# Modulation chunks gathered in one PSUM bank per batch instead of one bank use per chunk

## The chip, the cores and the metric

The kernel runs on one core of a Trainium2 chip. A core has a matrix engine (PE), a vector engine (DVE), a scalar engine (ACT), a general engine (POOL), an engine that only issues transfers here (SP), and 16 DMA engines. Matmul results go to banks of PSUM, which DVE and ACT read; this kernel has one bank for `pf`, three for `ps` and two double ones for `pd`. Everything else lives in SBUF. The metric is the device time of one execution in microseconds.

## The reference, cut to what matters

The program is two blocks one after the other, over 256 tokens of width 1024: two "hybrid" layers, and then two conditioned layers, each with an attention (neighbourhood attention, then grouped-query attention) and a mixture of 32 experts. The change concerns the conditioning vector of the second block:

```
c_act = jax.nn.silu(c)
for i in range(DEPTH):
    mod = c_act @ ada_w[i] + ada_b[i]
    sh1, sc1, g1, sh2, sc2, g2 = jnp.split(mod[:, None, :], 6, axis=-1)
    h = x * (1 + sc1) + sh1
    ...
    x = layer_norm(DEEPNORM_ALPHA * x + (1 + g1) * y, ln_g[i, 0], ln_b[i, 0])
    h = x * (1 + sc2) + sh2
    ...
    x = layer_norm(DEEPNORM_ALPHA * x + (1 + g2) * y, ln_g[i, 1], ln_b[i, 1])
```

`c` is one row of 1024 numbers; `ada_w` is 2 x 1024 x 6144. So `mod` is two vector-matrix products: 48 MB of weights for 12,288 results, six sections of 1024 for each layer.

## The kernel before, in words

The stages follow each other: hybrid layer 0 (0 to 166 us), hybrid layer 1 (to 322), the neighbourhood layer (to 490), its experts (to 945), the grouped-query layer (to 1090), and its experts. The modulation doesn't depend on the tokens, so it is worked off beside the other stages. Its weights are cut into 24 chunks of 2 MB, of 512 results each: chunk n belongs to layer n // 12, section n // 2 % 6, half n % 2.

A generator (`ada_cols`) makes two steps of a chunk: its load (L696), and its computation. Calls of `ada()` are spread over the layers, and a table (`ADA_PLAN`) says how many steps each call advances: the first four chunks lie in hybrid layer 0, 4 to 8 in layer 1 and at its end, 9 to 15 in the neighbourhood layer, 16 to 23 in the grouped-query layer. Within what these calls allow, a scheduler chooses the order on each engine when the program is built, and moves independent matmuls into gaps; only an instruction marked with `keep_in_program_order` stays where it is written. Loads go to buffers from a ring, so a load waits until the ones who used its buffer are done.

22 chunks are computed on PE (L706 to L727). The activated vector stands as the stationary operand `cact`, 128 x 32, each column the same. The 128 x 128 array is used as four column groups of 32: each group takes its 256 columns of the chunk and half of the depth (four matmuls of 128 rows), so 16 matmuls of 128x32 by 128x256 make a chunk. The profile counts two records for each, as the type is 32-bit. The result is 32 equal rows in each of the four groups, in the one bank `pf` that these uses share (L48: one buffer). DVE or ACT copies it to `parts` (L715). What remains is the tail (L718): two small matmuls with `sel`, a matrix of zeros and ones that adds the two depth halves and turns the row into columns, again through `pf`, and one DVE operation that adds the bias (and 1 for the scale sections) into `modc` (L723). A tail is held back until the next chunk has been copied (L716).

Two chunks (2 and 10, `ADA_ROWS`) are computed on DVE instead: four operations of 128x1024 that multiply the chunk by `crow` and sum (L701), and one that adds the bias (L702). `crow` is `c`, broadcast to all partitions by a transfer (L252) and activated by four ACT and eight DVE operations (L256 to L258).

`modc` is read by the feed of each layer, by `spread` (which makes rows out of a column vector with diagonal matrices, L747) and by `fold`, whose results POOL and DVE turn into the folded router weights in the same tile `parts` (L787, L788) and then into row sums by a matmul (L790). Split matmuls (`mm3`, L177) are those that multiply in three passes of high and low halves; transposes are L159, all other matmuls L162.

## Time and profile before

| | us |
|---|---|
| median of 3 runs | 1562.01 (1561.87 to 1565.70) |
| span of the profiled execution | 1560.8 |
| PE busy | 1231.1 (79%) |
| DVE busy | 569.4 (36%) |
| ACT busy | 356.6 (23%) |
| POOL busy | 236.6 (15%) |

The span goes from the first to the last instruction of the profiled execution; its own time is that span and about 1.2 us around it, if the median of the runs is taken for it. Busy times are sums over stages with different limits, so they don't say what bounds a stage. In the rows below, a group of matmuls is counted in records, and "[4.76 <-DVE parts L220]" means that the engine stood for 4.76 us before, and that a DVE instruction of line 220, writing the tile `parts`, released it.

### The profile page before, as it was taken

To read this page: it belongs to the slowest core of one execution; us is meant where nothing else is said; L and a number is where in the kernel's file an instruction comes from. 1 tells how busy PE (TensorE), PEld (TensorE's weight loads), DVE (VectorE), ACT (ScalarE), POOL (GpSimd) and SP (SyncE) were. 2 spreads that over 40 slices of the span, in tenths; PEclk is the share of its full clock that TensorE was granted. 3 is DMA by queue.
4 is the path that set the end of the run, shared out by engine and by line. 5 is a ranking of instruction groups with operands and counts; after the bars stand their busy time and mean duration, and the time that the engine had idled before them with its cause. 6 is when DMAs were issued, how large, how long until landed. Compare 5 with 4: busy or idle time off the path is not lost.

```text
span 1560.8 us, 24728 instructions
## 1 busy us (share of the span) xinstructions
PE 1231.1 (79%) x10584; PEld 789.8 (51%) x10584; DVE 569.4 (36%) x1258; ACT 356.6 (23%) x759; POOL 236.6 (15%) x283
## 2 busy tenths in 40 slices
PE   6898899999998986664877768889897764586774
PEld 6787788777967442321333326757543322243322
DVE  6677567555467210100111105877411100011113
ACT  5453443444442100000000004363100000010000
POOL 2721272122111200000000004320200000000000
PEclk9999999999999998876898889989999887798797
DMA  9436543468487999999999999575999999999995
GB/s 370 178 147 242 213 166 152 163 236 343 169 342 290 405 426 427 427 428 426 427 426 427 428 423 410 210 279 206 388 427 427 428 427 425 427 427 427 426 427 210
DMA packets 46705, 532.76 MB, mean 341 GB/s; under 512 B 7040, under 2 KB 10240, under 8 KB 15104
## 3 DMA queue, kind: packets, MB, share of 16 engines
q1 hardware_dynamic: 45440, 527.99, 82.2%
q10 hardware_dynamic: 1152, 3.15, 0.6%
q8 instruction: 85, 1.39, 0.4%
q14 instruction: 28, 0.23, 0.0%
HBM read 530.07 MB, written 1.05 MB: 340 GB/s over the span
## 4 chain that ended last, share of the span: by engine, by line
DMA 43%; PE 40%; DVE 9%; POOL 2%; ACT 2%; issue 2%; SPq 0%; DVEq 0%; ACTq 0%; POOLq 0%
DMA b<-in_moe_w_gate_up_dram 25%; DMA b<-in_moe_w_down_dram 16%; PE ps L162 14%; PE pd L177 9%; PE ps L177 8%; PE pf L162 3%; PE pd L162 3%; PE ps L159 3%; DMA b<-in_ada_w_dram 2%; DVE b L128 1%; ACT b L125 1%; POOL b L128 1%; POOL rs L196 0%; POOL rs L201 0%; DVE b L220 0%
## 5 line engine op out<-in xcount | busy, mean ns | idle before, releaser
L162 PE MATMUL ps<-b,b 128*32 128x256 f32 (+2 forms) x5248 | 484.6, 475 | 198.2 <-DMA b<-in_moe_w_gate_up_dram 138.9
L162 PEld LDWEIGHTS ps<-b,b 128*32 128x32 f32 (+1 forms) x5248 | 191.6, 120 | 432.1 <-issue 275.7
L177 PE MATMUL ps<-b,b 128*128 128x256 f32 (+1 forms) x1464 | 198.8, 295 | 6.6 <-DVE gates L565 5.6
L177 PEld LDWEIGHTS ps<-b,b 128*128 128x128 f32 x1464 | 186.7, 195 | 17.1 <-DVE gates L565 6.1
L177 PE MATMUL pd<-b,b 128*128 128x256 f32 (+2 forms) x1152 | 188.3, 320 | 4.6 <-ACT b L600 1.3
L177 PEld LDWEIGHTS pd<-b,b 128*128 128x128 f32 x1152 | 162.0, 196 | 25.3 <-issue 4.4
L128 POOL TENSOR_TENSOR b<-b,b 128x1024 fp32r<-128x1024 f32 (+2 forms) x46 | 115.5, 2517 | 348.2 <-ACT b L125 348.2
L125 ACT CAST b<-b 128x1024 fp32r<-128x1024 f32 (+1 forms) x124 | 126.1, 1035 | 160.2 <-PE ps L177 71.7
L226 ACT COPY b<-ps 128x256 f32<-128x256 f32 (+1 forms) x81 | 36.0, 449 | 456.4 <-PE ps L162 308.2
L128 DVE TENSOR_TENSOR b<-b,b 128x1024 fp32r<-128x1024 f32 x78 | 115.9, 1490 | 62.1 <-ACT b L125 57.0
L220 DVE COPY b<-ps 128x256 f32<-128x256 f32 (+1 forms) x71 | 36.2, 510 | 263.1 <-PE ps L162 214.1
L1115 POOL TENSOR_TENSOR b<-b,g 128x128 f32<-128x128 f32 x64 | 23.6, 399 | 595.1 <-PE ps L159 548.7
L1097 DVE SCALAR_TENSOR_TENSOR sl<-sl,ps 128x128 f32<-128x128 f32 x64 | 18.4, 288 | 248.4 <-ACT sl L1096 248.4
L159 PE MATMUL ps<-cst,b 128*128 128x128 f32 (+1 forms) x404 | 77.5, 302 | 39.7 <-DVE b L220 17.5
L159 PEld LDWEIGHTS ps<-cst,b 128*128 128x128 f32 (+1 forms) x404 | 45.3, 147 | 105.2 <-DVE b L220 34.7
L162 PE MATMUL pd<-b 64*128 64x512 f32 (+1 forms) x384 | 82.6, 552 | 15.4 <-DVE b L1145 12.9
L1145 DVE TENSOR_TENSOR b<-ps,parts 128x512 f32<-128x512 f32 x32 | 22.1, 692 | 180.8 <-PE ps L162 179.9
L162 PEld LDWEIGHTS ps<-b,x 128*128 128x128 f32 x512 | 68.3, 218 | 21.9 <-issue 18.4
L162 PE MATMUL ps<-b,x 128*128 128x128 f32 x512 | 72.2, 305 | 3.8 <-issue 1.6
L1096 ACT ACTIVATE sl<-ps 128x128 f32<-128x128 f32 x64 | 17.8, 278 | 236.9 <-PE ps L159 236.9
L162 PE MATMUL pf<-b,cact 128*32 128x256 f32 x704 | 56.0, 428 | 13.5 <-DVE modc L723 4.9
L162 PEld LDWEIGHTS pd<-b 64*128 64x128 f32 x384 | 34.3, 190 | 52.9 <-DVE b L1145 26.2
(304 smaller groups left out, 944.0 us busy)
## 6 DMA issues: line engine op xcount, KB each, us to landing
b<-in_moe_w_gate_up_dram SPq DMA_DIRECT2D x128, 2048.0 KB, 32.5
b<-in_moe_w_down_dram SPq DMA_DIRECT2D x62, 2048.0 KB, 35.3
b<-in_ada_w_dram SPq DMA_DIRECT2D x24, 2048.0 KB, 8.4
b<-in_w_in_dram SPq DMA_DIRECT2D x12, 2048.0 KB, 8.0
b<-in_na_w_qkv_dram SPq DMA_DIRECT2D x6, 2048.0 KB, 9.3
b<-in_gqa_w_qkv_dram SPq DMA_DIRECT2D x3, 2048.0 KB, 23.4
b<-in_w_out_dram SPq DMA_DIRECT2D x4, 1024.0 KB, 5.7
b<-in_w_out_dram SPq DMA_DIRECT2D x2, 2048.0 KB, 7.4
```

The lines of the kernel that those rows point to most:

```text
L125: S.copy(hi[:, s], v[:, s])
L128: (G if on_pool else e).tensor_tensor(lo[:, s], v[:, s], hi[:, s].bitcast(F32), OP.subtract)
L159: T.transpose(o, a, ident)
L162: return T.matmul(o, lhsT=a, rhs=b, start=start, stop=stop)
L177: T.matmul(o, lhsT=a[u], rhs=b[v], start=start and i == 0, stop=stop and i == 2)
L220: V.tensor_copy(o, i)
L226: S.copy(o, i)
L1096: S.activation(sl, ps[:, 0:128], AF.Tanh, scale=0.5)
L1097: V.scalar_tensor_tensor(sl, sl, 1.0, ps[:, 0:128], op0=OP.add, op1=OP.mult)
L1115: G.tensor_tensor(PG[:, t, :, du].rearrange("p q (e s) -> p q e s", e=2), P[:, t].rearrange("p (q e) s -> p q e s", q=2), g32[:, t, 4 * g: ...
L1145: V.tensor_tensor(do, ps, parts, OP.mult)
```

## The change

All 24 chunks are computed on PE, and chunks gather in batches: 0 to 6, 7 to 15, 16 to 23. The stationary operand is now a slice of a zero-padded tile `cz` (128 x 8 x 63) in which only column 31 holds the vector: the slice 31-s to 63-s has it in column s and zeros elsewhere. Chunk number s of a batch thus adds its result to row s of each column group and zeros to the others, and the bank `pf` is held from the first chunk of a batch to its last. Copy, tail matmuls and bias come once for each batch, in `flush`, with a wider `sel` (128 x 64); these two matmuls go to a `ps` bank. The 1 of the scale sections is added to the biases at the start. `crow`, its transfer and its activation go away. A call of `flush` is new at the end of the second hybrid layer; the other two stand where they stood.

```diff
-        if ADA_ROWS[n]:
-            w = w.rearrange("p (j k) -> p j k", j=4)
-            for j in range(4):
-                V.scalar_tensor_tensor(w[:, j], w[:, j], 1.0, crow, op0=OP.mult, op1=OP.mult, accum_out=o[:, j:j + 1])
-            V.scalar_tensor_tensor(o, o, one, b, op0=OP.add, op1=OP.add)
-            flush()
-            yield
-            return
         w = w.rearrange("p (k f) -> p k f", k=8)
-        part = parts[:, c * 256:c * 256 + 256]
-        first, ps = pin[0], PF()
+        s = len(batch)
+        if not s:
+            held[0] = PF()
+        batch.append(n)
         for k in range(4):
             for q in range(4):
                 kk, f0 = q % 2 * 4 + k, q // 2 * 256
-                i = mm(ps[32 * q:32 * q + 32, 0:256], cact[:, kk], w[:, kk, f0:f0 + 256], k == 0, k == 3)
+                i = mm(held[0][32 * q:32 * q + 32, 0:256], cz[:, kk, 31 - s:63 - s], w[:, kk, f0:f0 + 256],
+                       s == 0 and k == 0, n in ADA_LAST and k == 3)
-        evac(part, ps[:, 0:256])
-        flush()
...
-                mm(ps[:, 2 * i:2 * i + 2], a, sel, True, True)
-            V.scalar_tensor_tensor(o.rearrange("p (a i) -> p a i", i=2), ps[:, 0:4].rearrange("p (i a) -> p a i", i=2),
-                                   one, b.rearrange("p (a i) -> p a i", i=2), op0=OP.add, op1=OP.add)
```

The new `flush`:

```diff
+        n0, n = batch[0], len(batch)
+        acc, part, ps = held[0], parts[:, 0:256], PS()
+        evac(part, acc[:, 0:256])
+        for i in range(2):
+            mm(ps[:, i * 2 * n:(i + 1) * 2 * n].rearrange("p (a s) -> p a s", a=2), part[:, i * 128:i * 128 + 128],
+               sel[:, :, 0:n], True, True)
+        o = modc.rearrange("p l s k -> p (l s k)")[:, 4 * n0:4 * (n0 + n)]
+        b = col[:, K_ADA + 4 * n0:K_ADA + 4 * (n0 + n)]
+        V.tensor_tensor(o.rearrange("p (s a i) -> p s a i", a=2, i=2),
+                        ps[:, 0:4 * n].rearrange("p (i a s) -> p s a i", i=2, a=2),
+                        b.rearrange("p (s a i) -> p s a i", a=2, i=2), OP.add)
```

At the start:

```diff
-        nc.sync.dma_start(crow, p["c_2"].partition_broadcast(128))
-        for i in range(4):
-            c = crow[:, i * 256:i * 256 + 256]
-            S.activation(th, c, AF.Tanh, scale=0.5)
-            V.tensor_scalar(th, th, 0.5, 0.5, op0=OP.mult, op1=OP.add)
-            V.tensor_tensor(c, c, th, OP.mult)
...
-        V.tensor_copy(cact, csil[:, :, None].to_broadcast([128, 8, 32]))
+        V.memset(cz, 0.0)
+        V.tensor_copy(cz[:, :, 31], csil)
+        b = col[:, K_ADA:K_ADA + 96].rearrange("p (g n) -> p g n", g=4)[:, :, 8:24]
+        V.tensor_scalar(b, b, 1.0, None, op0=OP.add)
```

The order on PE changes in many places. The first shown is in the second hybrid layer, where PE waits for DVE's gates ahead of the next split matmuls (b_1585 and b_1573 are the layer's transposed input, b_2372 and b_2352 the weights of chunk 5, b_2567 and b_2541 those of chunk 6). Before:

```order
L177 MATMUL ps<-b_1585,b_83 128x256
L177 MATMUL ps<-b_1585,b_82 128x256 x2
L177 MATMUL ps<-b_1585,b_83 128x256
L177 MATMUL ps<-b_1585,b_82 128x256
L162 MATMUL pf<-b_2372,cact 32x256 x4
L177 MATMUL ps<-b_1585,b_82 128x256 [waits DVE_49]
```

Further on, before:

```order
L159 MATMUL ps<-cst,b_1553 128x128 [waits Activation_49]
L159 MATMUL ps<-cst,b_1553 128x128 x3
L159 MATMUL ps<-cst,b_1553 128x128 [waits DVE_49]
L159 MATMUL ps<-cst,b_1553 128x128 x3
L162 MATMUL pf<-b_2567,cact 32x256 [waits DMAHW7_49]
L162 MATMUL pf<-b_2567,cact 32x256 x15
L177 MATMUL ps<-b_1585,b_82 128x256 [waits DVE_49,Activation_49]
```

With the change:

```order
L177 MATMUL ps<-b_1573,b_82 128x256
L177 MATMUL ps<-b_1573,b_81 128x256
L162 MATMUL pf<-b_2352,cz 32x256 x10
L162 MATMUL pf<-b_2541,cz 32x256 [waits DMAHW0_49]
L162 MATMUL pf<-b_2541,cz 32x256 x15
L177 MATMUL ps<-b_1573,b_81 128x256 [waits DVE_49]
L177 MATMUL ps<-b_1573,b_82 128x256
```

Chunk 6's 16 matmuls moved from behind the next transposes to the gates' wait, and chunk 5 leaves ten there instead of four.

The second is the output projection of the first hybrid layer (pd is its result; b_1551 holds chunk 3 before, b_1521 and b_1539 chunks 2 and 3 now). Before:

```order
L177 MATMUL pd<-b_82,b_813 128x512 x2
L177 MATMUL pd<-b_83,b_813 128x512
L162 MATMUL pf<-b_1551,cact 32x256 x3
L177 MATMUL pd<-b_82,b_813 128x512 x4
L162 MATMUL pf<-b_1551,cact 32x256 x2
L177 MATMUL pd<-b_83,b_813 128x512
L177 MATMUL pd<-b_82,b_813 128x512 x2
```

With the change:

```order
L162 MATMUL pf<-b_1521,cz 32x256
L162 MATMUL pf<-b_1539,cz 32x256 x5
L162 MATMUL ps<-att,vd 64x128 x6
L162 MATMUL ps<-sgw,vn 64x128 x8
L177 MATMUL pd<-b_82,b_801 128x512
L177 MATMUL pd<-b_81,b_801 128x512 x2
L177 MATMUL pd<-b_82,b_801 128x512 x2
L177 MATMUL pd<-b_81,b_801 128x512 x2
L177 MATMUL pd<-b_82,b_801 128x512
L162 MATMUL pf<-b_1539,cz 32x256 x8
L177 MATMUL pd<-b_81,b_801 128x512 x2
L162 MATMUL pf<-b_1539,cz 32x256
```

Before, chunk 3's matmuls stood here in groups of 3 and 2, with 11 more behind the projection; now chunk 2's last one and chunk 3's stand here, in groups of 1 and 5 together, 8 and 1, with two more of 1 further on and 13 and 2 of chunk 2 ahead of them.

The third is the end of the neighbourhood layer, where the last head's products (64x256), the rows for the gate (diag) and the router's sums (parts, ones) follow each other. Before:

```order
L162 MATMUL pf<-cst,parts 128x2 [waits DVE_49]
L162 MATMUL pf<-cst,parts 128x2
L162 MATMUL ps<-b_3023,b_3022 64x256 [waits Activation_49]
L162 MATMUL ps<-b_3023,b_3022 64x256 x2
L159 MATMUL ps<-cst,b_3022 128x128 [waits PE_49]
L159 MATMUL ps<-cst,b_3022 128x128 x3
L162 MATMUL ps<-b_3023,b_3022 64x256 [waits DVE_49]
L162 MATMUL ps<-b_3023,b_3022 64x256 [waits Activation_49]
L162 MATMUL ps<-b_3023,b_3022 64x256 x2
L162 MATMUL ps<-diag,ones 128x128 [waits PE_49]
```

With the change:

```order
L162 MATMUL ps<-b_2996,b_2995 64x256 [waits DVE_49]
L162 MATMUL ps<-cst,parts 128x18 [waits DVE_49]
L162 MATMUL ps<-cst,parts 128x18
L162 MATMUL ps<-b_2996,b_2995 64x256 [waits Activation_49]
L162 MATMUL ps<-b_2996,b_2995 64x256 x2
L162 MATMUL ps<-diag,ones 128x128 [waits PE_49]
L162 MATMUL ps<-diag,ones 128x128
L162 MATMUL ps<-diag,ones 128x128 [waits DVE_49] x3
L162 MATMUL ps<-parts,ones 128x72 [waits DVE_49,PE_49]
```

The tail of the last chunk stood between two heads' products; now the flush's two matmuls stand there, one product later, and the sums' matmul has a wait for DVE that it did not have.

## Rows read from the trace of the kernel before

**Rows 1.** Part 4 of the page: the chain by engine, shares of the span.

```profile
DMA 43%; PE 40%; DVE 9%; POOL 2%; ACT 2%; issue 2%; SPq 0%; DVEq 0%; ACTq 0%; POOLq 0%
```

**Rows 2.** Windows, first MoE stage: length, engines' busy time, granted clock, DMA share, GB/s.

```profile
490.00:945.00 455.00, 330.81 (x3135) 159.25 (x3135) 66.49 (x202) 34.29 (x92) 26.77 (x55) 0.86 1.00 422
```

**Rows 3.** Tile pf: durations min/median/max; below, engines idle before it, us and times.

```profile
L162 PE MATMUL pf<-b,cact x704: 379/379/636, 66.0 to 1042.8; 128*32 128x256 f32 x176
...
  DVE parts L220: 17.9, 6
```

**Rows 4.** Timeline of PE, first layer: start, length, line, tiles, count, idle time before, releaser.

```profile
73.43 0.64 PE L162 MATMUL pf<-b,cact 128*32 128x256 f32 x8
78.83 3.64 PE L162 MATMUL pf<-b,cact 128*32 128x256 f32 x32 [4.76 <-DVE parts L220]
82.40 6.45 PE L177 MATMUL ps<-b,b 128*128 128x256 f32 x48
...
89.56 0.51 PE L162 MATMUL pf<-cst,parts 128*128 128x2 f32 x4
```

**Rows 5.** Timeline of PE, the same place in the second layer.

```profile
231.02 0.64 PE L162 MATMUL pf<-b,cact 128*32 128x256 f32 x8
237.29 7.37 PE L177 MATMUL ps<-b,b 128*128 128x256 f32 x48 [5.63 <-DVE gates L565]
```

**Rows 6.** Chain of waits in order of time, first layer: start, length, engine, line.

```profile
129.28 4.58 DVE b L701 x8
```

**Rows 7.** Timeline of PE, output projection of the first layer, start of the second.

```profile
147.64 0.73 PE L177 MATMUL pd<-b,b 128*128 128x512 f32 x2 [1.26 <-ACT b L600]
...
157.19 0.62 PE L162 MATMUL pf<-b,cact 128*32 128x256 f32 x4
...
163.86 1.50 PE L162 MATMUL pf<-b,cact 128*32 128x256 f32 x22
169.46 1.94 PE L159 MATMUL ps<-cst,att 128*128 128x128 f32 x8 [4.10 <-DVE att L456]
171.05 8.41 PE L177 MATMUL pd<-b,b 128*128 128x256 f32 x48
```

**Rows 8.** Timeline of PE, start of the neighbourhood layer to its first scores.

```profile
328.88 3.42 PE L162 MATMUL pf<-b,cact 128*32 128x256 f32 x32
...
334.06 11.66 PE L177 MATMUL pd<-b,b 128*128 128x256 f32 x95 [0.41 <-DVE b L297]
...
371.60 2.00 PE L162 MATMUL pd<-b 64*128 64x256 f32 x16
...
379.70 3.64 PE L162 MATMUL pf<-b,cact 128*32 128x256 f32 x32 [0.25 <-DVE modc L723]
...
384.94 0.65 PE L162 MATMUL ps<-b,b 128*64 128x256 f32 x2 [0.35 <-DVE b L220]
```

**Rows 9.** Timelines of POOL, DVE and PE, end of the neighbourhood layer.

```profile
459.26 0.67 POOL L787 TENSOR_TENSOR parts<-wge,fs 128x288 f32<-128x288 f32 x1 [22.65 <-PE pf L162]
...
460.28 0.67 DVE L788 TENSOR_REDUCE parts<-parts 128x36 f32<-128x288 f32 x1
...
464.67 0.34 PE L162 MATMUL ps<-parts,ones 128*128 128x72 f32 x2
```

**Rows 10.** Timeline of PE, grouped-query stage.

```profile
991.16 0.88 PE L162 MATMUL pf<-cst,parts 128*128 128x2 f32 x4 [3.42 <-DVE parts L220]
...
993.97 1.43 PE L159 MATMUL ps<-cst,b 128*128 128x128 f32 x8
...
1016.61 1.93 PE L162 MATMUL pf<-b,cact 128*32 128x256 f32 x32 [1.82 <-DVE modc L723]
```

**Rows 11.** Timeline of DVE, end of the rope for k.

```profile
990.30 0.48 DVE L938 TENSOR_TENSOR b<-b 128x128 f32<-128x128 f32 x2
```

**Rows 12.** Timeline of PE, first layer, before the waits above.

```profile
46.31 0.44 PE L159 MATMUL ps<-cst,b 128*128 128x128 f32 x2 [1.15 <-ACT cT L228]
```

**Rows 13.** Tile in_ada_w_dram: the 24 chunk loads, from issue to landing.

```profile
DMA to landing us min/median/max: 7.6/8.4/26.2
```

More of the change, by code (lines that the diff above doesn't have):

```diff
@@ L17 @@
 C_ID, C_TRIU, C_STRICT, C_CM, C_INV, C_IOTA, C_AX, C_D4, C_D8, C_SEL, C_THR, NCONST = (
-    0, 128, 256, 384, 768, 792, 824, 952, 956, 964, 966, 973)
+    0, 128, 256, 384, 768, 792, 824, 952, 956, 964, 1028, 1035)
 R_MQ, R_KN, R_KR, R_SG, R_SB, R_BQ, R_BK, R_N = 0, 96, 160, 192, 448, 704, 768, 832
@@ L26 @@
 RSQ_SEED = 1597463007.0
-ADA_ROWS = [int(i) for i in '001000000010000000000000']
+ADA_LAST = (6, 15, 23)
 ADA_PLAN = (1,2,1,3,0,2,2,2,2,3,4,10,1,0,2,1,4)
@@ L154, in tile_hybrid_then_moe @@
     strict = cst[:, C_STRICT:C_STRICT + 128]
-    sel = cst[:, C_SEL:C_SEL + 2]
+    sel = cst[:, C_SEL:C_SEL + 64].rearrange("p (a s) -> p a s", a=2)
     iota32 = cst[:, C_IOTA:C_IOTA + 32]
@@ L261, in start @@
         V.tensor_tensor(csil, csil, col[:, K_C:K_C + 8], OP.mult)
-        V.tensor_copy(cact, csil[:, :, None].to_broadcast([128, 8, 32]))
-    cact = const.tile([128, 8, 32], F32, name="cact")
-    crow = const.tile([128, D], F32, name="crow")
+        V.memset(cz, 0.0)
+        V.tensor_copy(cz[:, :, 31], csil)
+        b = col[:, K_ADA:K_ADA + 96].rearrange("p (g n) -> p g n", g=4)[:, :, 8:24]
+        V.tensor_scalar(b, b, 1.0, None, op0=OP.add)
+    cz = const.tile([128, 8, 63], F32, name="cz")
     def rope(eng, x1, x2, sin, cos, t1, t2, t3, t4):
@@ L680, in hybrid, with ada_chunk @@
         ada()
+        if l:
+            flush()
     modc = const.tile([128, 2, 6, 8], F32, name="modc")
     parts = const.tile([128, 512], F32, name="parts")
-    pend = []
+    batch, held = [], [None]
     def flush():
-        while pend:
-            pend.pop()()
-    def ada_cols(l, sec, c, n):
-        b0 = K_ADA + (l * 6 + sec) * 8 + c * 4
-        o, b, one = modc[:, l, sec, c * 4:c * 4 + 4], col[:, b0:b0 + 4], 0.0 if sec in (0, 3) else 1.0
+        if not batch:
+            return
+        n0, n = batch[0], len(batch)
+        assert batch[-1] in ADA_LAST
+        acc, part, ps = held[0], parts[:, 0:256], PS()
[8 more added lines that the diff above has]
+                        b.rearrange("p (s a i) -> p s a i", a=2, i=2), OP.add)
+        batch.clear()
+        held[0] = None
+    def ada_chunk(n):
         w = chunk(adab[0] and adab[0]())
@@ L711, in ada_cols @@
                 kk, f0 = q % 2 * 4 + k, q // 2 * 256
-                i = mm(ps[32 * q:32 * q + 32, 0:256], cact[:, kk], w[:, kk, f0:f0 + 256], k == 0, k == 3)
-                if first and k == q == 0:
+                i = mm(held[0][32 * q:32 * q + 32, 0:256], cz[:, kk, 31 - s:63 - s], w[:, kk, f0:f0 + 256],
+                       s == 0 and k == 0, n in ADA_LAST and k == 3)
+                if pin[0] and k == q == 0:
                     tc.keep_in_program_order(i)
-        evac(part, ps[:, 0:256])
-        flush()
-        def tail():
-            ps = PF()
-            for i in range(2):
-                a = part[:, i * 128:i * 128 + 128]
-                mm(ps[:, 2 * i:2 * i + 2], a, sel, True, True)
-            V.scalar_tensor_tensor(o.rearrange("p (a i) -> p a i", i=2), ps[:, 0:4].rearrange("p (i a) -> p a i", i=2),
-                                   one, b.rearrange("p (a i) -> p a i", i=2), op0=OP.add, op1=OP.add)
-        pend.append(tail)
         yield
@@ L730, in ada_steps @@
         for n in range(24):
-            yield from ada_cols(n // 12, n // 2 % 6, n % 2, n)
+            yield from ada_chunk(n)
     adab, pin = [None], [False]
@@ L1282, in _consts @@
     c[:, C_STRICT:C_STRICT + 128] = i[:, None] < i[None, :]
-    c[:, C_SEL:C_SEL + 2] = (i[:, None] % 32 == 0) & (i[:, None] // 64 == np.arange(2))
+    s = np.arange(64)[None, :]
+    c[:, C_SEL:C_SEL + 64] = (i[:, None] % 32 == s % 32) & (i[:, None] // 64 == s // 32)
     c[:, C_THR:C_THR + 7] = 32 * np.arange(1, 8)
@@ L1326, in _layout @@
         w = g["ada_w_2"][l, :, s * D + c * 512:s * D + c * 512 + 512]
-        if ADA_ROWS[n]:
-            w = w.T.reshape(4, 128, D).transpose(1, 0, 2)
-        else:
-            w = w.reshape(8, 128, 512).transpose(1, 0, 2)
-        a["ada_w_2"][n] = w.reshape(128, 4 * D)
+        a["ada_w_2"][n] = w.reshape(8, 128, 512).transpose(1, 0, 2).reshape(128, 4 * D)
     a["consts"] = _consts()
```

3 lines of the change are left out of this document (1 added, 2 removed).

## The prediction

> **What bounds the kernel now.** I read the chain of waits by engine first, to see what a saved microsecond of PE is worth. DMA holds 43% of the chain, PE 40%, DVE 9% [rows 1]. The table by stage splits that: in the first MoE stage (490 to 945 us) the DMA engines are busy for 1.00 of the time [rows 2], and the second, after 1090, is built alike. So nothing that this change does on PE shortens a MoE stage by itself. But a stage that ends earlier ahead of it lets its weights start earlier, and I pass such a saving on one to one. What counts is therefore the two hybrid layers (0 to 322), the neighbourhood layer (322 to 490) and the grouped-query stage.
>
> Next I read the modulation's own bank, pf. Its 704 records take 379 ns each in the middle, four at a time on four column groups. PE sat idle ahead of it for 17.9 us, six times, until DVE had copied a result out [rows 3]. That is the serial hand-over which the change takes out; beside it the tails go. It is no forecast: a PE that stops waiting here may wait for something else two matmuls later, so each place is read by itself in the timeline.
>
> **The first hybrid layer.** The second chunk's 32 records stand until 78.83, 4.76 us idle, for the copy of the first; then 48 split matmuls (L177) follow from 82.40 to 88.85 [rows 4]. In the changed order the second chunk waits for its load alone. What is late next are the gates. The same place in the second layer shows them: chunk records at 231.02, L177 from 237.29 after 5.63 us for DVE's gates [rows 5]. The two layers lie 231.02 - 73.43 = 157.59 apart, so the gates should be there at 237.29 - 157.59 = 79.7. The 48 would then start 2.7 earlier, but off a long idle, 7.37 instead of 6.45 us [rows 4, 5]: gain 2.7 - 0.9 = **1.8**. Above is 4.76 if the gates come too, below 0.
>
> Tails: one costs 0.51 us on PE [rows 4], about 0.1 of it beside the next group by the starts, so I take 0.4. Five of them stand in the two hybrid layers: gain **2.0** (bounds 0 and 2.6).
>
> DVE's chunk in this layer is 4.58 us on the chain [rows 6]. PE shows of it only short waits, the clearest 1.26 us at 147.64 [rows 7], because it had other work. Bounds 1.3 and 4.6; near the smaller one I take **2.0**.
>
> Against that, all of chunks 2 and 3 now stands on PE in the output projection, in groups of 26, 4, 12, 16, 2, 2 and 2 records (the order shows half of each, since a matmul of this type runs as two records). A group of 4 costs 0.62 us, of 8 0.64, of 32 1.93 [rows 4, 7, 10]: 0.06 a record, but never under 0.6. That makes 1.6 + 0.6 + 0.7 + 1.0 + 3 x 0.6 = 5.7. Before, two groups stood there (0.62 and about the same), while the other 22 records ran at 163.86 ahead of a 4.10 us wait for the next norm and were free [rows 7]. Cost 5.7 - 1.2 = **4.5**; if all of it fills waits, 1, and 5.7 at most.
>
> Here a rule speaks against the change. The trace shows the floor of 0.6 us for a group that should take 0.24 (4 of 0.06) [rows 7]. The Trainium skill, TensorEngine Tiling (Array Packing), section Key Properties, says that changing the tiling mode, and not merely the tile, empties the array; that agrees with the floor. By the rule every scattered group pays; by 0.06 a record alone the groups above would cost 3.8 instead of 5.7, and the sum would be 1.9 lower.
>
> **The second hybrid layer.** Here 52 records stand in the wait for the gates: 52 x 0.06 = 3.1 of 5.63 us [rows 5]. They take with them the 32 records of chunk 6 that stood 18 us further on, on PE's path, 1.93 as any 32 at full speed [rows 10], and the idle left is 2.5, so the 48 after it may run nearer to 6.45 than to 7.37: 0.4 of the 0.9. Gain **2.3** (1.9 to 2.8). Chunk 4 is cut into six groups (+1.4) and chunk 7 into three instead of five (-1.1): cost **0.3**. At its end the first flush and chunk 8 stand ahead of the transposes. Before, chunk 8 ran at 328.88 for 3.42 us, at half speed (1.2 of 2.4 GHz, by the 1.93 of other chunks), while DVE prepared the operands, and the 95 split matmuls from 334.06 ran at full speed, 11.66 / 95 = 0.123 each [rows 8]. Without that filler they may start at half speed: 48 cost 8.41 at 171.05 after such a wait [rows 7] against 48 x 0.123 = 5.9, so 2.5. The transposes behind the chunk come up to 1.5 sooner. I take a cost of **1.5** (from a gain of 1.5 to a loss of 2.5).
>
> On that filler the row and a rule agree about the direction and not the size. The half-speed start above is the row. The Trainium skill, TensorE: Matmul & The Clock Gate, section HAM oscillation — how this bites in real kernels, says that a waiting gap in PE's work makes the next stretch start cold. By the rule the whole 2.5 would be lost, and the sum 1.0 worse.
>
> **The neighbourhood layer.** Seven tails go (-2.8). Chunk 10 comes from DVE, where it was hidden, to PE (32 records, +1.9). Its neighbour at 379.70 ran at half speed, 3.64 against 1.93 [rows 8, 10]; half of that difference comes back (-0.8). At the end the flush has a chain of its own. Before, POOL's product for the router's weights stood ready to run, 22.65 us behind on the bank's scratch alone, 0.67 us, and DVE's sum over it 0.67 [rows 9]. Now its factors come out of the flush: a copy, two matmuls like a tail's (0.51 [rows 4]), an add, three small folds, then those two steps (1.34). I estimate 3 us for the chain, and the matmul that takes it has stood about 3.7 us behind the old sums (464.67 against 460.28 + 0.67) [rows 9]. I take +1.3, with 0 and 3 as bounds. Chunk 11's load is issued after chunk 10's last matmul instead of after DVE; I count nothing for it, since the first scores and their softmax hide a usual load (0 to 16, worked out with the third rival). Together -0.4, a gain of **0.4**.
>
> **The grouped-query stage.** Waits for the bank: 3.42 us at 991.16, then the tail, and the transposes of k at 993.97 [rows 10]. DVE's rope for k ends at 990.30 + 0.48 = 990.8 [rows 11]; this is what is late next, so the transposes gain 3.2 and not all of the idle ahead of them. Behind it 1.82 at 1016.61 [rows 10], of which I count half, 0.9, since ACT's and DVE's softmax set the pace there; six tails, 2.4. Against: two groups more of 2 matmuls, 0.7 beyond their records, and a flush chain as above, 1.3. Gain **4.5** (1 to 8).
>
> **Sum.** -1.8 - 2.0 - 2.0 + 4.5 - 2.3 + 0.3 + 1.5 - 0.4 - 4.5 = -6.7. The row of c goes too, with its broadcast, four tanh on ACT and eight DVE operations in the first 45 us. Most of it lies beside the first layer's projections; one wait of PE for ACT, 1.15 at 46.31, follows it closely [rows 12]. Between 0 and 1.15 I take 0.6. So -7.3 on the profiled span of 1560.8, which gives 1553.5; the median of the runs shown, 1562.01, is 1.2 above the span, so **1554.7 us**. The flushes' evacuation, the zero fill of 128x504 and the added 62 columns of constants lie beside loads at the start; without that cover they cost under 1 us.
>
> **Rivals.**
> *The waits only change their name.* The rope at 990.8 comes a little later with DVE's new order, the gates too, and the small groups take the tails' 9 us. For it: DVE follows PE by tenths of a microsecond at both places [rows 5, 11]. Against it: the 3.42 and 4.76 us have DVE's copy as releaser, not these. Only the second layer's 2.3 and half of the tails stay, and the output projection's 4.5 eats them: 1561.
>
> *All of it comes back.* The gates follow (4.76 in place of 1.8), DVE's 4.6 count in full with the projection's groups in its waits (cost 1), the clock stays up: 3.0 + 2.6 + 3.5 + 1.5 = 10.6 more, 1544.
>
> *Slower: a chunk's load arrives too late.* Every chunk's matmuls stand in PE's program order, and whatever is behind waits too. Place: chunk 11 in the neighbourhood layer, whose buffer is now given back by PE. A chunk's load takes 8.4 us in the middle and 26.2 at most [rows 13]. Between chunk 10's last matmul and it stand the first scores, their softmax, the transposes and the first product with v: 371.60 to 384.94 before, less the 3.64 us of the chunk that stood among them [rows 8], so 9.7 us. A usual load is hidden; the longest makes PE stand 26.2 - 9.7 = 16.5 us. From a landing of about 17 us the stall eats all 7.3 us, and from 22 us, with 12 of stall, the kernel is slower: 1554.7 + 12 = 1567; at the longest 1571. Against it: the median, not the worst, is what a load outside the MoE stages takes.
>
> **How the numbers follow.** Forecast 0.5 (1549 to 1558), waits renamed 0.26 (1558 to 1564), all back 0.12 (1541 to 1549), late load 0.12 (1564 to 1571). The range is **1545 to 1566**. No change means within 0.3% of 1562.0, that is 1557.3 to 1566.7; less than this a measurement of this kernel hardly tells from no change. Faster: 0.12 and most of 0.5: 0.54. Same: the rest of the forecast and nearly all of the renamed waits: 0.33. Slower: the late load and a little of the renamed waits: 0.13.
>
> **What would show it.** PE's idle time to DVE's parts under 2 us, and no stand between the first two chunks; the gates' wait there at 79 to 80. The second layer's 32 records inside the gates' wait and none near 255. The transposes of k near 990.8 or with DVE's rope as releaser. More PE time in the first layer's output projection by about 4 us. The forecast is wrong if the grouped-query stage isn't 3 us shorter, if the projection's groups cost nothing, or if PE waits for a chunk's load for more than 3 us anywhere but at the start of the grouped-query stage.

## The result, and the profile after

The changed kernel takes 1574.32 us (median of 5 runs) against 1565.70 for the kernel before in the same session (5 runs, the three of the table above among them): the ratio is 1.0065, 95% interval 1.0048 to 1.0082. It is slower by about 10 us by the ratio and by 8.6 by the two medians, where 7 us faster was forecast, and the time lies above the range. Of the 19.6 us between it and the forecast 3.7 are the base's, which was 1562.01 by the first three runs. In the profiled execution the span is 1572.5 us, 11.7 more than before, and the mean granted clock of PE is 0.900 instead of 0.905.

What the change set out to remove is gone. The tile pf in the changed kernel, with what its engines waited for:

```profile
L162 PE MATMUL pf<-b,cz x768: 379/379/637, 64.4 to 1054.6; 128*32 128x256 f32 x192
...
  issue: 17.3, 46
  DMA b<-in_ada_w_dram: 4.6, 6
```

64 records more than before (chunks 2 and 10), as long each, and no wait for DVE's parts, where there were 17.9 us [rows 3]. The chain by engine, of the changed kernel:

```profile
DMA 43%; PE 20%; DVE 5%; ACT 1%; issue 1%; POOL 0%; SPq 0%; DVEq 0%; ACTq 0%
```

PE's share has halved against [rows 1] and the kernel is slower: the chain is one way back through work that ends nearly together, and which way is taken says little about what a place costs. So I compare the same work in both timelines. The 11.7 us come about like this (start of one piece of work to the next, before and after; MoE is a layer's mixture of experts):

| stretch | before | after | difference |
|---|---|---|---|
| to the end of the neighbourhood layer's 95 split matmuls | 345.72 | 346.17 | +0.45 |
| to its router sums | 118.95 | 121.21 | +2.26 |
| to the first expert matmul | 34.92 | 33.68 | -1.24 |
| first MoE, to the grouped-query stage's x transposes | 454.31 | 456.30 | +1.99 |
| grouped-query stage, to the second MoE's first matmul | 146.58 | 154.35 | +7.77 |
| second MoE, to the end of the span | 460.32 | 460.79 | +0.47 |

There is one trace for each kernel, which limits how finely this can be read. A kernel below ("Only the place") has the same order on PE as the kernel before up to the first expert matmul, and this matmul starts at 503.32 us in its trace and at 499.59 in the trace before. So the rows of 0.5 to 2.3 us can't be told from what differs between two runs of one order; the 7.77 can, and the experiments make it come and go.

PE of the changed kernel, the same place in the two hybrid layers as [rows 4, 5] (start, length, line, tiles, count, idle time before, releaser):

```profile
71.77 2.37 PE L162 MATMUL pf<-b,cz 128*32 128x256 f32 x40
78.17 7.51 PE L177 MATMUL ps<-b,b 128*128 128x256 f32 x48 [4.04 <-DVE gates L561]
...
231.61 3.22 PE L162 MATMUL pf<-b,cz 128*32 128x256 f32 x52
237.49 7.51 PE L177 MATMUL ps<-b,b 128*128 128x256 f32 x48 [2.66 <-DVE gates L561]
```

Both places went the way that was forecast. The first layer's 48 wait for the gates alone, which come at 78.17 and not at 79.7, and end 3.2 us earlier (85.68 for 88.85) where I took 1.8. The second layer hides 52 records in that wait, but its 48 still take 7.51 us, and the 0.4 that I took off for them didn't come.

PE at the start of the grouped-query stage, which is where most was lost:

```profile
957.36 1.97 PE L159 MATMUL ps<-cst,x 128*128 128x128 f32 x8 [6.04 <-DVE x L768]
959.26 3.38 PE L162 MATMUL pf<-b,cz 128*32 128x256 f32 x32
962.57 1.09 PE L159 MATMUL ps<-cst,x 128*128 128x128 f32 x8
963.42 11.76 PE L177 MATMUL pd<-b,b 128*128 128x256 f32 x96
```

Chunk 16's 32 records stand between the first eight x transposes and the rest, after PE has stood idle for 6.04 us ahead of them. In the kernel before they were done ahead of the transposes, most of them in that idle time:

```profile
950.36 3.61 PE L162 MATMUL pf<-b,cact 128*32 128x256 f32 x32 [3.74 <-DMA b<-in_ada_w_dram]
953.90 1.53 PE L159 MATMUL ps<-cst,x 128*128 128x128 f32 x12
```

They held these transposes up a little: DVE's operations that write x start 2.11 us ahead of the transposes there (951.79) and 0.86 us in the changed kernel (956.50). Counted from those operations, the stage is 6.5 us longer and the first MoE 3.2, with the same sum.

In the changed kernel the split matmuls start 6.06 us after the first transposes instead of 3.97 (957.87 before). The issues of chunk loads on SP's queue, before and then after, show the second effect (start, stretch over which they were issued, count):

```profile
954.02 0.33 SPq L696 DMA_DIRECT2D b<-in_ada_w_dram  x1
971.76 0.33 SPq L696 DMA_DIRECT2D b<-in_ada_w_dram  x1
984.39 28.13 SPq L696 DMA_DIRECT2D b<-in_ada_w_dram  x3
```

```profile
962.71 14.72 SPq L706 DMA_DIRECT2D b<-in_ada_w_dram  x2
998.83 5.51 SPq L706 DMA_DIRECT2D b<-in_ada_w_dram  x2
1035.01 3.90 SPq L706 DMA_DIRECT2D b<-in_ada_w_dram  x2
```

A chunk's load takes the buffer of an earlier chunk, so the load that waited for chunk 16 goes out at 962.71 instead of 954.02, and those after it are late in turn. The chunks that they bring then miss the gaps in which they stood. PE of the changed kernel, from the transposes of k on:

```profile
992.75 0.53 PE L159 MATMUL ps<-cst,b 128*128 128x128 f32 x2 [4.00 <-DVE b L931]
...
995.56 6.53 PE L177 MATMUL pd<-b,b 128*128 128x256 f32 x37
1002.02 1.93 PE L162 MATMUL pf<-b,cz 128*32 128x256 f32 x32
...
1008.15 1.93 PE L162 MATMUL pf<-b,cz 128*32 128x256 f32 x32
...
1021.19 2.08 PE L162 MATMUL pd<-b 64*128 64x256 f32 x8 [1.84 <-ACT b L359]
1025.12 1.97 PE L159 MATMUL ps<-cst,b 128*128 128x128 f32 x8 [1.86 <-DVE b L222]
1027.02 2.78 PE L162 MATMUL pf<-b,cz 128*32 128x256 f32 x20
...
1075.04 4.52 PE L177 MATMUL pd<-b,b 128*128 128x512 f32 x12
...
1091.55 4.57 PE L177 MATMUL ps<-b,b 128*128 128x512 f32 x12
```

Nothing fills the waits of the first softmax (1.84 and 1.86; before, a whole chunk stood in this stretch, at 1016.61 [rows 10]). Four chunks stand from 1027 on, where PE waits for little. And some rows run at half speed, 1.2 of 2.4 GHz, for a part of their time: behind the wait for the transposes of k, 37 in 6.53 us is 0.176 each against 0.123 [rows 8], at a granted clock of 0.68. The 12 at 1075.04 and the 12 at 1091.55 take 4.52 and 4.57 us where others of this form take 3.00.

Of the 7.77 us, 4.41 lie ahead of the stage's router sums (116.78 us from the x transposes for 112.37) and 3.36 behind them, 3.1 of these in the two slow groups. The two are no part of the place: in the run "Chunk 8 into the gap", chunk 16 stands in the same place and they run at full speed.

In the neighbourhood layer the same happened on a smaller scale:

```profile
332.12 14.05 PE L177 MATMUL pd<-b,b 128*128 128x256 f32 x95 [0.78 <-DVE b L293]
...
369.88 3.64 PE L162 MATMUL pf<-b,cz 128*32 128x256 f32 x58
373.45 2.00 PE L162 MATMUL pd<-b 64*128 64x256 f32 x16
...
385.78 2.79 PE L162 MATMUL pf<-b,cz 128*32 128x256 f32 x24 [0.76 <-DMA b<-in_ada_w_dram]
```

The 95 split matmuls run in part at half speed without the chunk right ahead of them (14.05 for 11.66 [rows 8], at a granted clock of 0.80 for 1.00), chunk 10 stands ahead of the first scores (58 records at 369.88), and the next chunk waits for its load.

### The profile page after: what moved, and what is told of

It reads as the page before. It is cut to its first block, busy times and chain, and to the rows that moved or that the text cites. A ratio compares the mean times of both kernels' runs of the same rounds, so it can differ in the third digit from the quotient of the medians.

```text
span 1572.5 us, 24621 instructions
## 1 busy us (share of the span) xinstructions
PE 1235.9 (79%) x10572; PEld 791.5 (50%) x10572; DVE 551.1 (35%) x1207; ACT 352.5 (22%) x744; POOL 238.4 (15%) x283
## 4 chain that ended last, share of the span: by engine, by line
DMA 43%; PE 20%; DVE 5%; ACT 1%; issue 1%; POOL 0%; SPq 0%; DVEq 0%; ACTq 0%
DMA b<-in_moe_w_gate_up_dram 25%; DMA b<-in_moe_w_down_dram 19%; PE ps L162 12%; PE pd L177 2%; PE pd L162 2%; PE ps L159 2%; PE pf L162 1%; PE ps L177 1%; DVE rs L197 0%; ACT b L125 0%; DVE b L220 0%; DVE lst L759 0%; POOL b L128 0%; DVE b L128 0%; DVE rs L194 0%
## 5 line engine op out<-in xcount | busy, mean ns | idle before, releaser
L177 PEld LDWEIGHTS pd<-b,b 128*128 128x128 f32 x1152 | 165.9, 201 | 22.3 <-issue 5.5
L162 PE MATMUL pf<-b,cz 128*32 128x256 f32 x768 | 62.1, 407 | 1.3 <-DMA b<-in_ada_w_dram 1.2
```

What stands on the lines that cost most here:

```text
L162: return T.matmul(o, lhsT=a, rhs=b, start=start, stop=stop)
L177: T.matmul(o, lhsT=a[u], rhs=b[v], start=start and i == 0, stop=stop and i == 2)
```

## The experiments

The first theory, "places", says: the loss isn't in the new matmuls but in where chunks came to stand in PE's order, chunk 16 above all, through the work behind them and the loads that wait for their buffers. The first rival, "work", puts it on the matmuls that were added to PE, with their small groups; the second, "flush", on the chains that a batch adds at a stage's end. Two later rivals are named where they come up. Times are medians; the ratio is to runs of the kernel before on the same chip, whose median lay between 1563.84 and 1565.70 us, so where two experiments are compared the ratios are the safer measure.

**All chunks on PE, nothing else.** The kernel before with chunks 2 and 10 on PE, each chunk with its own bank use, tail and scatter:

```
-ADA_ROWS = [int(i) for i in '001000000010000000000000']
+ADA_ROWS = [int(i) for i in '000000000000000000000000']
```

> The kernel before with one edit: chunks 2 and 10 are computed on PE too, each chunk still with its own bank use, copy and tail. In the built order chunk 16 then stands behind the first eight transposes of the grouped-query layer, as in the changed kernel. Theory 'places' (time is lost where chunk matmuls left PE's waits, above all chunk 16 and what its buffer holds back): slower than before by 6 to 11 us, the transposes at the start of the grouped-query layer 3 us late, chunk 18's load 8 us late. Theory 'flush' (the chain copy, two matmuls, add, fold, router weights at the ends of the stages costs the time): no more than 3 us slower than before, since nothing is flushed in a batch here. Theory 'work' (two more chunks on PE): 4 to 6 us slower, all of it in the first 490 us.

Measured: 1572.15 us, ratio 1.0050 (1.0032 to 1.0069). By itself this seems to speak for "work": no batch, and most of the loss is there. But its trace has chunk 16 behind the first eight transposes too:

```profile
957.89 1.97 PE L159 MATMUL ps<-cst,x 128*128 128x128 f32 x8 [6.04 <-DVE x L775]
959.78 2.78 PE L162 MATMUL pf<-b,cact 128*32 128x256 f32 x32
```

So it changes two things, and the next runs part them. Its stage from these transposes to the second MoE's first matmul takes 150.33 us, 3.8 more than before, and its first expert matmul comes 4.2 later (503.80): about half of the loss lies in either part.

**Chunk 16 first.** The changed kernel, with chunk 16's matmuls written ahead of the feed in the program (the plan's numbers), and the projection's instructions queued behind them on PE (`issue_after` keeps what is in its block behind the instruction named):

```
-ADA_PLAN = (1,2,1,3,0,2,2,2,2,3,4,10,1,0,2,1,4)
+ADA_PLAN = (1,2,1,3,0,2,2,2,2,3,4,10,2,0,1,1,4)
...
-        pkv = proj_wide(hT, split, wkv, feed, G, rest)
+        with tc.issue_after(last_mm[0]):
+            pkv = proj_wide(hT, split, wkv, feed, G, rest)
```

> The changed kernel with one edge added: the PE work of the grouped-query projection is queued behind chunk 16's matmuls, as it stood before the change. Theory 'places': 6 to 10 us faster than the changed kernel (2.8 at the transposes, 4 to 5 because chunks 20 and 21 stand in the softmax waits again, 1 to 3 of clock), 1564 to 1568, about level with before. Theory 'flush': under 3 us faster than the changed kernel, 1571 to 1575. Theory 'work': the same.

Measured: 1565.08 us, ratio 1.0011 (0.9999 to 1.0023): 9.2 us come back. Its PE in the grouped-query stage:

```profile
950.97 1.93 PE L162 MATMUL pf<-b,cz 128*32 128x256 f32 x32
956.88 1.63 PE L159 MATMUL ps<-cst,x 128*128 128x128 f32 x12 [3.98 <-DVE x L769]
...
1007.34 1.04 PE L159 MATMUL ps<-cst,b 128*128 128x128 f32 x8
...
1010.10 1.93 PE L162 MATMUL pf<-b,cz 128*32 128x256 f32 x32
...
1017.18 3.10 PE L162 MATMUL pf<-b,cz 128*32 128x256 f32 x28
```

Chunk 16 is free in the wait for the layer norm, and two later chunks stand in the softmax waits. The stage takes 142.7 us (956.88 to 1099.62), 3.8 less than before; the traced run took 1561.92 us, 3.2 below this kernel's median. The flush is in it all the same, and the matmul with the sums waits 0.18 us for it: "flush" does not explain the loss. The stage from its first x transposes on:

| from the first x transposes to | before | changed | chunk 16 first | before, chunk 16 late (below) |
|---|---|---|---|---|
| the first split matmuls | 3.97 | 6.06 | 3.53 | 6.06 |
| the transposes of k | 40.07 | 35.39 | 34.46 | 35.66 |
| those of q | 55.33 | 55.52 | 50.46 | 56.33 |
| the output projection | 98.52 | 100.16 | 92.15 | 100.85 |
| the second MoE's first matmul | 146.58 | 154.35 | 142.74 | 154.75 |

**DVE keeps its two chunks.** The changed kernel, with chunks 2 and 10 computed on DVE as before, and 22 batched on PE:

```
+ADA_ROWS = [int(i) for i in '001000000010000000000000']
...
+        if ADA_ROWS[n]:
...
+                V.scalar_tensor_tensor(w[:, j], w[:, j], 1.0, crow, op0=OP.mult, op1=OP.mult, accum_out=o[:, j:j + 1])
```

> The changed kernel with chunks 2 and 10 on DVE as before (their sums are added to the bias column ahead of the flush; the zero-padded tile and the selecting matrix are cut to 40 and 18 columns so that the row of c fits). Chunk 16 stays behind the transposes. Theory 'places': 2 to 4 us faster than the changed kernel, all of it in the neighbourhood layer, where chunk 11 stands in the softmax waits again; the grouped-query stage as long as in the changed kernel. Theory 'work': 7 to 10 us faster, level with before. Theory 'flush': no difference of more than 2 us.

Measured: 1569.09 us, ratio 1.0032 (1.0020 to 1.0044): 5.2 below the changed kernel. The router sums of the neighbourhood layer come 5.8 us earlier (461.57), of which 1.8 are left at the first expert matmul (499.25); on the way two groups of 12 matmuls (462.46 and 479.06) take 4.59 us each, in part at half speed, for 3.02 and 3.01 in the changed kernel. The grouped-query stage is as long as in the changed kernel, 154.35. "Places" had all of the gain in the neighbourhood layer; in these two traces the rest is in the MoE stages (first MoE 453.45 for 456.30), and why is open.

**Chunk 8 into the gap.** The changed kernel with chunk 8 queued behind the first eight x transposes of the neighbourhood layer, to keep PE busy ahead of the 95 split matmuls:

```
+        def chunk8():
+            with tc.issue_after(last_tr[0].ins):
+                ada(1)
```

> The changed kernel with chunk 8's 16 matmuls queued behind the first eight transposes of the neighbourhood layer, in the wait for the operands, as before the change. Theory 'places': the first 96 split matmuls take 11.8 us instead of 14.05, the end of the neighbourhood layer is 2 to 3 us earlier, the kernel 2 to 3 us faster. Theories 'flush' and 'work': the 96 may be faster, but the wait for the flush at the layer's end takes it back: under 1 us.

Measured: 1572.45 us, ratio 1.0050 (1.0037 to 1.0063). It failed in its aim. PE of this kernel:

```profile
320.75 1.93 PE L164 MATMUL pf<-b,cz 128*32 128x256 f32 x32
...
326.89 0.93 PE L161 MATMUL ps<-cst,x 128*128 128x128 f32 x4 [3.20 <-ACT b L232]
...
328.92 13.86 PE L179 MATMUL pd<-b,b 128*128 128x256 f32 x95 [0.60 <-DVE b L295]
...
1077.12 3.03 PE L179 MATMUL pd<-b,b 128*128 128x512 f32 x12
...
1092.15 2.99 PE L179 MATMUL ps<-b,b 128*128 128x512 f32 x12
```

The chunk runs at once, and 3.20 us of idle time still lie between it and the 95, which run in part at half speed again. In the kernel before the chunk ran until 332.30, 1.8 us ahead of them [rows 8]. By the medians the kernel is 1.9 us below the changed kernel, but the two intervals overlap. The last two lines are the groups that were slow in the changed kernel. Chunk 16 stands behind the first eight transposes here too, the stage reaches its router sums as late (116.72 us), and yet it takes 150.58 us for 154.35.

**Only the place, in the kernel before.** The kernel before, with nothing of the change; chunk 16's matmuls are queued behind the first eight x transposes, as they stand in the changed kernel:

```
             pin[0] = False
-            ada()
+            with tc.issue_after(last_tr[0].ins):
+                ada()
```

> The kernel before, all its arithmetic and its chunks on PE and DVE as they were; only the 16 matmuls of chunk 16 are put behind the first 8 x transposes of the grouped-query stage, as they stand in the changed kernel (its load and everything that follows it in the buffers then falls as the pool decides). Theory 'places' (the changed kernel lost its time because chunk 16 stands behind the transposes): this kernel alone loses most of the 9.2 us that putting chunk 16 back saved, so 1570 to 1574 us, and the stage from its x transposes to the second MoE's first matmul, 146.6 us before, takes 151 to 155. Theory 'work' (the loss is in the matmuls, selectors and flushes of the change): within 2 us of the kernel before.

Measured: 1572.72 us, ratio 1.0060 (1.0038 to 1.0081). The place alone costs as much as the whole change did. Its PE, at the start of the neighbourhood layer and in the grouped-query stage:

```profile
331.31 1.93 PE L164 MATMUL pf<-b,cact 128*32 128x256 f32 x32
...
336.19 13.15 PE L179 MATMUL pd<-b,b 128*128 128x256 f32 x95 [0.34 <-DVE b L299]
...
956.79 1.97 PE L161 MATMUL ps<-cst,x 128*128 128x128 f32 x8 [6.04 <-DVE x L777]
958.68 3.39 PE L164 MATMUL pf<-b,cact 128*32 128x256 f32 x32
...
1026.06 1.54 PE L161 MATMUL ps<-cst,b 128*128 128x128 f32 x6 [3.25 <-DVE b L224]
```

The stage reads like that of the changed kernel up to the first softmax, though its chunks still have their own tails: 154.75 us, the chunk's next load at 962.14, and the same unfilled waits in the first softmax (2.07 at 1020.73 and 3.25).

The first two lines are from a stretch where this kernel's order is that of the kernel before. There chunk 8 took 3.42 us and the 95 took 11.66 [rows 8], at granted clocks of 0.54 and 1.00; here 1.93 and 13.15, at 1.00 and 0.87. The sum is 15.08 both times, 1.5 more than both at full speed (1.93 + 11.66): the same half speed fell on the chunk in one run and on the 95 in the other.

**All chunks on PE, chunk 16 first.** The first experiment with the edit of the second:

> The kernel before with all 24 chunks on PE, each with its own bank, tail and scatter, and chunk 16 held ahead of the first x transposes. Against the run with the chunks on PE and no such hold (1572.15 us) it tells the place again; against the changed kernel with chunk 16 first (1565.08) it tells what one bank and one flush for each batch are worth by themselves. Theory 'places': 1572.15 - 9 = 1563 us, and the batch is then worth nothing to 2 us either way, since 21 tails fewer are paid back by three flush chains and by groups that no longer stand in waits. The prediction's own terms (tails 2.0 + 2.8 + 2.4, scatter waits 2.3, against flushes of 1.3 + 1.3) would have the batch gain some 5 us, so 1570 here. Theory 'work': as without the hold, 1572.

Measured: 1568.43 us, ratio 1.0034 (1.0020 to 1.0048). Against it the changed kernel with chunk 16 first is 3.4 us faster: that is what one bank and one flush for each batch are worth with chunk 16 first, less than the 5 of the prediction's own terms and more than the nothing that I wrote for "places". With chunk 16 late they are worth nothing: the changed kernel is then 2.2 us slower than the one with all chunks on PE (1574.32 for 1572.15, with intervals that overlap).

The other half of the expectation failed too. The place is worth 3.7 us here (2.5 by the ratios) and not 9; the stage takes 147.34 us for 150.33. Both chunk orders differ from those of the other pairs here, so what one chunk's place costs depends on what else stands in the stage, and that part of "places" is not worked out.

**Both repairs.** The changed kernel with chunks 2 and 10 on DVE and chunk 16 first:

> The changed kernel with both of its repairs at once: chunks 2 and 10 stay on DVE (1569.09 us alone, 5.2 below the changed kernel) and chunk 16 is held ahead of the first x transposes (1565.08 alone, 9.2 below). If the two places are independent, as theory 'places' has it (one before the first MoE, one behind it, with its weight stream between them), 1574.3 - 5.2 - 9.2 = 1560 us, 4 to 5 below the kernel before. If the first MoE's weight stream takes back what the earlier stages gain (theory 'memory'), 1563 to 1565. Theory 'work' has no gain from the hold: 1569.

Measured: 1561.59 us, ratio 0.9986 (0.9970 to 1.0001), 12.7 below the changed kernel; against the run with chunks 2 and 10 on DVE alone the place is worth 7.5. The two repairs add up to within 2 us (5.2 + 9.2 = 14.4), so "memory", the rival by which the first MoE takes back what is gained ahead of it, is not needed. The interval just touches no change, so I don't call it faster than the kernel before.

**Only chunk 2 on DVE.** The same with one digit changed, so that chunk 10 is on PE:

```
-ADA_ROWS = [int(i) for i in '001000000010000000000000']
+ADA_ROWS = [int(i) for i in '001000000000000000000000']
```

> As the last, but only chunk 2 stays on DVE; chunk 10 is on PE as in the changed kernel. It tells whose the 5.2 us before the first MoE are. If chunk 10's 16 matmuls in the first scores' waits cost them (theory 'places': it pushes chunk 11 out of those waits, +3.4 us at the second half's first projection), the time is that of the changed kernel with chunk 16 first, 1565, within 1 us. If it is chunk 2 (16 more matmuls and a load of its own between the two hybrid layers), it is 1560 to 1561. The prediction's terms (-2.0 for DVE's chunk 2, +1.9 for chunk 10) would have 1567.

Measured: 1569.16 us, ratio 1.0037 (1.0025 to 1.0049), above all three expectations. So chunk 10 on PE costs 7.6 us here, and all of it is there at the first expert matmul (505.60 for 497.99 in the last run). It is no price of chunk 10 alone: with chunk 2 on PE too the time is 1565.08, 4.1 us less, which none of the theories has. Its PE:

```profile
367.62 3.64 PE L163 MATMUL pf<-b,cz 128*32 128x256 f32 x58
...
385.51 1.92 PE L163 MATMUL pf<-b,cz 128*32 128x256 f32 x10 [3.80 <-DMA b<-in_ada_w_dram]
```

The 58 records of chunks 9 and 10 stand 2.3 us earlier than in the changed kernel, and PE then stands for 3.80 us until the next chunk's load lands. With chunk 10 on DVE (the run before), the third load was issued by 338 (323.51 + 14.80), since DVE gave the buffer back; with it on PE that load is issued from 371 on, when PE has reached the chunks. SP's issues of chunk loads in the run before, then in this one, and from issue to landing of the last three here:

```profile
323.51 14.80 SPq L714 DMA_DIRECT2D b<-in_ada_w_dram  x3
```

```profile
321.21 4.65 SPq L714 DMA_DIRECT2D b<-in_ada_w_dram  x2
371.30 20.79 SPq L714 DMA_DIRECT2D b<-in_ada_w_dram  x3
```

```profile
DMA to landing us min/median/max: 9.4/14.2/19.2
```

They go out behind three weight loads (347.06 to 369.90) and take 14.2 us, 12.2 in the changed kernel, so an earlier start of the layer brings the chunk no sooner: it lands at 385.5 here and at 385.8 there.

**Chunk 10 moved.** Two runs of the changed kernel with chunk 16 first, in which the plan sets chunk 10 later; all chunks stay on PE. First its load and its matmuls behind the scores:

```
-ADA_PLAN = (1,2,1,3,0,2,2,2,2,3,4,10,2,0,1,1,4)
+ADA_PLAN = (1,2,1,3,0,2,2,2,2,3,2,12,2,0,1,1,4)
```

> The changed kernel with chunk 16 first (1565.08 us) and one number of the plan moved: chunk 10's 16 matmuls are no longer traced ahead of the neighbourhood attention's first scores but behind them, so that they stand in the softmax waits, where chunk 11 stood in the kernel before. All 24 chunks stay on PE, in the same banks, with the same flushes. Theory 'places': the first scores come 1.8 us earlier (one chunk of 1.9 us less before them), the second half's first projection, 394.7 there, at 391 to 392, and the whole at 1561 to 1563. Theory 'load' (the first half ends when the loads into the two buffers that chunks 9 and 10 hold have landed, wherever chunk 10 stands): the first scores come earlier but chunk 11 or 12 waits longer, and the whole stays at 1565. Theory 'work': 1565 too, without such a wait.

Measured: 1567.00 us, ratio 1.0019 (1.0009 to 1.0029). The second half's first projection came at 391.94, as "places" had it, and PE waited 1.99 us for a chunk's load, as "load" had it, but the whole is no shorter: 1.9 us longer by the medians and 1.3 by the ratios, whose intervals overlap. Chunks pushed into the second half leave PE waiting for DVE there (1.19 us at 461.55). Then with the load ahead (3,3,11 in the plan for 3,2,12):

> As the last, but with chunk 10's load still ahead of the scores and its matmuls set between the first half's three score groups; chunks 11 and 12 then leave the softmax waits and stand in the second half's projections, where PE has no waits. Theory 'places': the first half gains its 1.8 us before the scores and the 3.8 us of chunks 11 and 12 in the softmax waits (a first projection of the second half at 388 to 390 against 394.7), and pays 3.8 us for the same chunks in the second half: 1563 to 1565. Theory 'load': nothing waits for a load here, and the sums of the first stage's end come 4 us earlier, 1561. Theory 'work': 1565.

Measured: 1566.28 us, ratio 1.0010 (0.9998 to 1.0021). The second half's first projection came at 387.82 instead of 394.69, 6.9 us earlier and without a wait for a load; at the router sums 0.7 is left, and the first expert matmul is 3.2 us later (503.59 for 500.39), which is no more than two traces of one order differ by there:

```profile
466.88 4.62 PE L177 MATMUL pd<-b,b 128*128 128x512 f32 x12
...
483.49 4.58 PE L177 MATMUL ps<-b,b 128*128 128x512 f32 x12
```

Both groups took 3.0 with chunk 10 unmoved (3.03 and 3.00 us). The ratio is that of the run without the move (1.0011). So "places" names the first half's gain rightly and is wrong on the whole: what a layer gains in its first half it pays in its second, where four chunks stand in PE's path, and in two half-speed groups. Why such groups run at half speed in some runs and not in others is open; the one at the same place took 4.58 us in "Only the place" (483.25) and 3.00 in the kernel before (481.00), in the same order.

## Why the prediction was wrong, point by point

**Where it failed.** The step "The grouped-query stage", gain 4.5, assumed that chunk 16 still stands in the idle time ahead of the transposes. The built order of the changed kernel already showed it behind the first eight of them; I read the order for the places where a wait went, and not for this chunk, which waited for nothing but its load. Measured: a loss of 7.8, and my own sign of being wrong, a stage not 3 us shorter, came. With the chunk in its old place the stage gains 3.8, so the sum of this step's terms (waits, tails, against groups and flush) was right to 0.7 us. The terms themselves were not, and that they cancel is luck: the transposes of k come 34.46 us after those of x instead of 40.07, 5.6 earlier where I took 3.2, and the rest of the stage is 1.8 longer (108.28 for 106.51) where I took 1.3 off.

**The chunk's price and the sum.** In ratios to the kernel before (0.1% is 1.56 us): all chunks on PE with chunk 16 first +5.3 us (1.0034), the batch on top of it +1.7 (1.0011), its place lost +10.2 (1.0065). So, in this order of steps, the place cost 8.5, the batch gained 3.6, and taking DVE's two chunks onto PE cost 5.3. In other orders the prices are others: the place costs 9.4 in the kernel before (1.0060), 7.2 with DVE's chunks kept (1.0032 for 0.9986), and 2.5 with all chunks on PE and no batch (1.0050 for 1.0034). That the place makes most of the loss is shown, by taking it out of the changed kernel and by putting it into the kernel before; why it costs less in the third pair is open.

Against the forecast's -7.3, by the stretches of the table above: to the end of the 95 -2.4 was forecast and +0.45 came, the rest of the neighbourhood layer -0.4 and +1.0, the MoE stages 0 and +2.5, the grouped-query stage -4.5 and +7.8. That is 19.0 us off, 12.3 of them in the grouped-query stage. Why the first MoE took 2 us more is open: in the runs here it took 453.5 to 456.5 us, with no order in it that I could find.

**The start of the neighbourhood layer.** Cost 1.5, bounds -1.5 and 2.5: the 95 lost 2.4, nearly the bound, and the transposes came only 1.7 us sooner, with PE idle for 3.90 us behind the first twelve. The end of the 95 is 0.45 later; with the hybrid layers' terms (a net 3.9) less this 1.5 it should have been 2.4 earlier. The Trainium skill, TensorE: Matmul & The Clock Gate, section HAM oscillation — how this bites in real kernels, says that matmuls behind a wait of PE start cold. By it the whole 2.5 would have been lost, and the 2.4 of the 95 agrees with that rather than with my 1.5. But in "Only the place" the 95 took 13.15 in the order of the kernel before, so 1.5 of the 2.4 may be lost without the change too.

**The neighbourhood layer.** Gain 0.4; measured +2.26 to the router sums, and -1.24 from there on. Chunk 10 costs about its 1.9: the first scores come 1.4 later behind the 95 (27.28 us for 25.88). The term that was off is "I count nothing" for the load of the chunk that takes chunk 10's buffer: that chunk waits (0.76 in the changed kernel, 3.80 in the run with chunk 2 alone on DVE), and from the scores to the second half's first projection the changed kernel takes 1.5 more (21.59 for 20.09).

**The hybrid layers.** Layer 0, whose terms add to about -1 with its share of the tails and the row of c, ended 0.8 earlier (168.66 for 169.46). Layer 1's hidden records and small groups are as forecast, but from its start to the next x transposes it is only 0.9 shorter (154.95 for 155.88), where its terms with two tails give 2.8. What the sum had no term for is chunk 8 itself: its 32 records, which stood in the wait behind these transposes, stand ahead of them in three groups of 0.64, 0.62 and 1.50 us (312.90, 315.51 and 322.18). The first layer's output projection groups cost about what was said, 6.0 us by the starts for 5.7, three of 2 records each like this one:

```profile
147.62 0.62 PE L162 MATMUL pf<-b,cz 128*32 128x256 f32 x2
```

**The rivals.** "A chunk's load arrives too late" had the right mechanism and the right chunk in the neighbourhood layer: PE gives the buffer back late, and the load, 12.2 us behind three weight loads, makes PE wait. But its price there was 0.8 us and not 16, and its larger effect was in the grouped-query stage, where no chunk waits for a load: the chunks no longer stand in the gaps that they could not reach in time. "The waits only change their name" is right on the names, as PE stands 4.04 us for the gates and 4.00 for the rope where it stood 4.76 and 3.42 for the copies, and wrong on the time: both places come earlier behind their start, and with chunk 16 in its place the stage kept the gain. "All of it comes back" is wrong by the result.

## What to carry to other kernels

A chunk of filler work has two places: one in its engine's order and one in its buffer's queue. Whoever changes what it waits for should read in the built order where each filler now stands, the ones outside the edit too, and which load waits for its buffer; one chunk that stands 9 us later cost 8 to 9 us in the changed kernel and in the kernel before, and 2.5 to 3.7 where the other chunks stood otherwise. When fillers leave a wait, ask what stands in it next, since idle time was often paid for twice here: by itself and by half speed after it. And before a microsecond or two of one trace is put down to the change, compare two traces of one order: here they differed by up to 3.7 us ahead of the first MoE.

## What the runs showed of the hardware that was not expected

Two or four records between other matmuls cost as much as eight: 0.62 us for 2 and 0.63 for 4 (129.61 of the changed kernel), 0.62 to 0.64 for 8. And a start at half speed wasn't bought off here by work somewhere in the gap: 32 records that ended 6.2 us ahead of the 95 (322.68 to 328.92) left them at 13.86 us; 32 that ended 1.8 us ahead of them (332.30 to 334.06), with transposes between, at 11.66 [rows 8]. Those 32 had themselves run at half speed (3.42 us); in the same order in another run they took 1.93, and the 95 behind them 13.15.
